# Three more landing buffers for gathered expert rows, shared with the tiles that empty the accumulators

## The chip, the core and the metric

The kernel runs on one core of a Trainium2 chip. The metric is the device time of one execution in microseconds (us), as the median of several runs. The engines are TensorE (PE in the profile), VectorE (DVE), ScalarE (ACT), GpSimd (POOL) and SyncE (SP). SP issues the plain loads and stores, POOL issues the indirect DMAs (gathers), and 16 DMA engines carry both.

## The reference

One layer of a decoder trunk over 1024 tokens of width 1024: three mixers, a product-key expert layer (PEER), a gated per-layer embedding, a final norm. The change lies in PEER, where every token has 8 x 16 = 128 chosen experts, each with an input row `u` and an output row `v` of 1024 floats:

```
def block(args):                      # 128 tokens at a time
    xb, ib, gb = args
    act = jax.nn.gelu(jnp.einsum('td,thkd->thk', xb, u[ib]), approximate=False)
    return jnp.einsum('thk,thkd->td', act * gb, v[ib])
```

`u` and `v` have 16384 rows each (64 MB).

## The kernel before

The 1024 tokens are two halves of four blocks of 128 tokens. In the first half of the program the mixers run; the `u` rows of the first half's four blocks are gathered behind the second half's mixer work. The stage that matters here comes after that and runs from about 2570 to 4266 us.

**The scattered part.** `experts_out` computes the `v` side of six blocks without a gather. For six blocks, in two passes of three, it multiplies a matrix of weights W (experts by tokens, mostly zeros) with all of `v`. A pass has three chunks of 43, 43 and 42 steps; each step `i` loads 128 rows of `v` (`raw`, tag `vr`, four buffers, L1161, 512 KB) and runs six products of 128x512 into six accumulator banks `pair` (L1165; the trace has 12 matmuls a step). While a chunk runs, `scatter` builds the W of the next one: DVE makes one-hot tiles A8, B8 (L1085) and Bs (L1097) for 8 tokens, PE multiplies them in groups of 24 small matmuls (L1064), ACT copies the product into W (L1066). A chunk has 48 such groups.

**The gathered part.** At the same time `gathered()` works on the second half of the tokens: `experts_in` gathers 128 `u` rows per token of four blocks and reduces each with the token's own vector `hft` (L1021); `experts_rows` gathers the `v` rows of the two blocks that the passes leave out and adds them up (L1038). `rows` hands out the landing buffers in turn: three of tag `ug` in the pool `up` and, in this stage, two more, `ug0` and `ug1`, in the pool `vp`. One gather is 128 rows of 4 KB, 512 KB.

**The order.** DVE keeps the order in which the code is written. In every step from the 17th on, `feed` takes the scatter's share and then 3.2 gathered rows (`RATE`), so 240 steps take the 768 gathers. PE's, ACT's, POOL's and SP's orders are chosen by the scheduler.

**The end of a pass.** `finish` copies the six accumulator banks into three tiles `es` of 4 KB a partition (L1127, ACT), then `add_block` transposes each (L1113), copies it back (L1115) and adds it to the residual (L1117), a piece per step of the next chunk. The next pass's matmuls write the same banks. The three `es` tiles have a place of their own in `vp` and are used twice in the stage, at the end of each pass.

Of the kernel before, what the change touches and what calls it, by code (L numbers as in the profile page):

```python
# [10 lines left out]
F32 = mybir.dt.float32  # L11
# [10 lines left out]
P = 128  # L22
D = 1024
# [5 lines left out]
UB = 3  # L29
# [27 lines left out]
def tile_trunk(ctx, tc, xT, pT, w_in, w_tm, w_br, w_q, keys, peer_u, peer_v,  # L57
# [5 lines left out]
    up = ctx.enter_context(tc.tile_pool(name="up", bufs=1))  # L63
# [6 lines left out]
    def nm(s):  # L70
        cnt[0] += 1
        return f"{s}_{cnt[0]}"

    def st(shape, dt=F32, tag="t", bufs=1, pool_=None):
        p = pool_ or pool["r" if tag in ("mg", "rw", "keyt") or tag.startswith("p_") else "s"]
        return p.tile(list(shape), dt, tag=tag, name=nm(tag), bufs=bufs)
# [26 lines left out]
    turn = {"pj": 0, "g": 0, "s": 0, "t": 0, "u": -1}  # L103
# [45 lines left out]
    def pj(shape=(P, T)):  # L149
        turn["pj"] = 1 - turn["pj"]  # L150
        return bank(turn["pj"], shape)
# [94 lines left out]
    def to_cols(rows, n):  # L246

        s = tmp([16, T])[0:n]
        A.copy(out=s, in_=rows)
        tp = pg((P, NC, 16))  # L250
        for c in range(NC):
            PE.transpose(tp[:, c, 0:n], s[:, c * P:c * P + P], ident[0:n, 0:n])
        return tp[:, :, 0:n]
# [94 lines left out]
    def small_rows(hf, H):  # L348
# [31 lines left out]
        def bc(t, rows=8):  # L380
            return t.unsqueeze(2).to_broadcast([rows, NC, P])
# [609 lines left out]
    def route_slots(res, pj=pg):  # L991

        for r in res:
            tp = pj((P, 2, P))
            for i in range(2):
# [2 lines left out]
                A.copy(out=t, in_=tp[:, i])  # L998
                r[2 + i] = t

    def rows(table, ii, extra):

        for s in range(P):
            turn["u"] = (turn["u"] + 1) % (len(extra) + UB)
            m = turn["u"]
            p, tag = (up, "ug") if m < UB else extra[m - UB]
            x = st([P, D], tag=tag, bufs=UB if m < UB else 1, pool_=p)
            G.indirect_dma_start(out=x, out_offset=None, in_=table,  # L1008
                                 in_offset=bass.IndirectOffsetOnAxis(ap=ii[:, s:s + 1], axis=0))
            yield s, x  # L1010

    def experts_in(hf, tb, r, hpool, extra):


        gt, ii = r[0], r[1]
        gt = gt.rearrange("p a b -> p (a b)")
        act = st([P, P], tag="act", bufs=1, pool_=up)
        hft = st([P, D], tag="hft", bufs=1, pool_=hpool)
        SY.dma_start(out=hft, in_=hfd[hf, tb])
        for s, ug in rows(peer_u, ii, extra):  # L1020
            V.tensor_tensor_reduce(out=ug, in0=ug, in1=hft, scale=1.0, scalar=0.0,  # L1021
                                   op0=ALU.mult, op1=ALU.add, accum_out=act[:, s:s + 1])
            if s == P - 1:
                A.activation(out=act, in_=act, func=AF.Gelu)
                V.tensor_tensor(out=gt, in0=act, in1=gt, op=ALU.mult)
                r.append("weighted")
            yield

    def experts_rows(r, extra, sums):

        gt, ii = r[0].rearrange("p a b -> p (a b)"), r[1]
        o = st([P, D], tag="hft", bufs=1, pool_=up)
        sums.append(o)
        for s, vg in rows(peer_v, ii, extra):
            if s == 0:
                V.tensor_scalar(out=o, in0=vg, scalar1=gt[:, 0:1], scalar2=None, op0=ALU.mult)
            else:
                V.scalar_tensor_tensor(out=o, in0=vg, scalar=gt[:, s:s + 1], in1=o, op0=ALU.mult, op1=ALU.add)  # L1038
            yield
# [64 lines left out]
    def add_block(vp, hf, tb, e, xt=None):  # L1104

        src = xmd[hf, :, :, tb * P:tb * P + P].rearrange("k p t -> p k t")
        if xt is None:
            xt = vp.tile([P, KT, P], F32, tag="vr", name=nm("xt"), bufs=VB)
            SY.dma_start(out=xt, in_=src)
        for d in range(2):  # L1110
            tp = pj((P, NC, P))
            for k in range(4):
                PE.transpose(tp[:, k, :], e[:, d * T + k * P:d * T + k * P + P], ident)  # L1113
            f = e[:, d * T:d * T + T].rearrange("p (k t) -> p k t", k=NC)
            A.copy(out=f, in_=tp)  # L1115
            yield
            V.tensor_tensor(out=xt[:, 4 * d:4 * d + 4], in0=f, in1=xt[:, 4 * d:4 * d + 4], op=ALU.add)  # L1117
        SY.dma_start(out=src, in_=xt)
        yield

    def finish(vp, blocks, acc):

        es = []
        for b in range(3):
            e = vp.tile([P, D], F32, tag="es", name=nm("es"), bufs=3)
            for d in range(2):
                A.copy(out=e[:, d * T:d * T + T], in_=acc[b][d])  # L1127
            es.append(e)
        yield
        for e, (hf, tb) in zip(es, blocks):  # L1130
            yield from add_block(vp, hf, tb, e)

    def tile_w(n):
        return [pool[p].tile([P, (QM, CHUNKS[0][1] - QM)[k], 3 * P], F32, tag=f"W{k}", name=nm("W"), bufs=1)
# [2 lines left out]
    def experts_out(vp, W, passes, gen, then, last):  # L1137
# [7 lines left out]
        for n, (p, c) in enumerate(chunks):  # L1145
# [33 lines left out]
            if c == len(CHUNKS) - 1:  # L1179
                end = finish(vp, [x[0:2] for x in passes[p]], acc)  # L1180
                next(end)
# [54 lines left out]
    def opened(name, side="left"):  # L1236
        es = ExitStack()
        return es, es.enter_context(tc.tile_pool(name=name, bufs=1, side=side, reuse_waits="tile"))
# [109 lines left out]
    v2, vp = opened("v2", "right")  # L1348
# [3 lines left out]
    sums = []  # L1352

    def gathered():
        ex = [(vp, "ug0"), (vp, "ug1")]
        yield from experts_in(1, 0, r1[0], vp, ex)
        yield from experts_in(1, 1, r1[1], vp, ex)
        yield from experts_in(1, 2, r1[2], vp, ex)
        yield from experts_rows(r1[2], ex, sums)
        yield from add_block(vp, 1, 2, sums[0])  # L1360
        yield from experts_in(1, 3, r1[3], vp, ex)
        yield from experts_rows(r1[3], ex, sums)

    es = []
# [24 lines left out]
    blocks = [[(0, tb, r0[tb]) for tb in range(3)], [(0, 3, r0[3]), (1, 0, r1[0]), (1, 1, r1[1])]]  # L1389
    with tc.manual_schedule(engines={mybir.EngineType.DVE}):  # L1390
        experts_out(vp, W, blocks, gathered(), then, last())
        for _ in add_block(vp, 1, 3, sums[1]):
            pass
# [98 lines left out]
```

## Time and profile before

| what | us |
|---|---|
| time, median of three runs | 4431.17 |
| the three runs | 4431.17, 4423.65, 4438.31 |
| the profiled execution's own time | 4443.27 |
| its span from first to last instruction | 4441.4 |
| PE busy in the span | 4001.2 |
| DVE busy | 3306.1 |
| POOL busy | 1679.9 |
| ACT busy | 1176.4 |

The mean granted TensorE clock is 0.944 of full speed. The profile reads 1018.30 MB moved by DMA, 671.17 MB of it on the gathers' queue. The span is 1.9 us shorter than the time of its execution, which itself lies 12.1 us above the median. Busy shares are averages over stages with different limits; matmuls are pipelined, so a busy PE is not a PE at its peak.

### The profile page before, as it was taken

To read this page: it belongs to the slowest core of one execution; us is meant where nothing else is said; L and a number is where in the kernel's file an instruction comes from. 1 tells how busy PE (TensorE), PEld (TensorE's weight loads), DVE (VectorE), ACT (ScalarE), POOL (GpSimd) and SP (SyncE) were. 2 spreads that over 40 slices of the span, in tenths; PEclk is the share of its full clock that TensorE was granted. 3 is DMA by queue.
4 is the path that set the end of the run, shared out by engine and by line. 5 is a ranking of instruction groups with operands and counts; after the bars stand their busy time and mean duration, and the time that the engine had idled before them with its cause. 6 is when DMAs were issued, how large, how long until landed. Compare 5 with 4: busy or idle time off the path is not lost.

```text
span 4441.4 us, 55491 instructions
## 1 busy us (share of the span) xinstructions
PE 4001.2 (90%) x20506; PEld 2492.5 (56%) x20506; DVE 3306.1 (74%) x6607; ACT 1176.4 (26%) x2192; POOL 1679.9 (38%) x1299
## 2 busy tenths in 40 slices
PE   8999999999778988898978998999999999998967
PEld 5677787777556655556744744444444444443435
DVE  5333346549999777878879899888888888886755
ACT  3343425432325412314403201111111111110023
POOL 0000000000146665564460005566666666665620
PEclk9999999999889998899999999999999999999988
DMA  2212122242268898887783237899998999999953
GB/s 92 93 56 72 55 95 72 85 138 91 100 233 303 292 347 281 282 308 277 242 316 132 84 124 268 312 343 347 337 335 319 354 336 338 331 340 380 365 196 102
DMA packets 326081, 1018.30 MB, mean 229 GB/s; under 512 B 33584, under 2 KB 81072, under 8 KB 325552
## 3 DMA queue, kind: packets, MB, share of 16 engines
q0 software_dynamic: 184320, 671.17, 42.3%
q1 hardware_dynamic: 141488, 343.58, 22.1%
q8 instruction: 161, 2.64, 0.2%
q14 instruction: 112, 0.92, 0.1%
HBM read 992.84 MB, written 21.77 MB: 228 GB/s over the span
## 4 chain that ended last, share of the span: by engine, by line
DVE 18%; issue 17%; PE 16%; DMA 14%; POOL 10%; ACT 1%; SPq 0%; POOLq 0%; DVEq 0%; ACTq 0%
POOL ug L1008 10%; DMA ug<-in_peer_u_dram,ii 7%; PE bank L214 6%; DVE ug L1021 5%; DMA ug<-in_peer_v_dram,ii 5%; PE pair L1165 3%; DVE A L1085 1%; DVE hft L1038 1%; DVE Bs L1097 1%; PE bank L205 1%; DVE p_pk L940 1%; DVE mg L936 1%; DVE wlo L183 1%; PE pair L1064 1%; PE bank L1064 1%
## 5 line engine op out<-in xcount | busy, mean ns | idle before, releaser
L1008 POOL DMA_INDIRECT ug<-in_peer_u_dram,ii x1024 | 1348.3, 1317 | 2386.3 <-DVE ii L979 1387.5
L1165 PE MATMUL pair<-vr,W 128*128 128x512 f32 x3072 | 1414.3, 612 | 17.7 <-DMA vr<-in_peer_v_dram 17.7
L1021 DVE CUSTOM_DVE_ANT_0 ug<-ug,hft 128x1024 f32<-128x1024 f32 x1024 | 1226.4, 1220 | 272.1 <-DMA ug<-in_peer_u_dram,ii 240.3
L1165 PEld LDWEIGHTS pair<-vr,W 128*128 128x128 f32 x3072 | 579.4, 195 | 672.5 <-issue 651.7
L214 PE MATMUL bank<-hi,wlo 128*128 128x512 f32 x1552 | 623.9, 402 | 35.9 <-DVE wlo L183 34.8
L214 PE MATMUL bank<-hi,whi 128*128 128x512 f32 x1552 | 632.5, 409 | 12.2 <-ACT hi L182 4.2
L214 PE MATMUL bank<-lo,whi 128*128 128x512 f32 x1552 | 623.0, 402 | 0.1
L183 DVE TENSOR_TENSOR wlo<-raw,whi 128x1024 fp32r<-128x1024 f32 (+1 forms) x276 | 327.2, 1186 | 336.4 <-ACT whi L182 318.4
L182 ACT CAST whi<-raw 128x1024 fp32r<-128x1024 f32 (+1 forms) x276 | 282.2, 1023 | 1057.8 <-PE bank L214 618.9
L1066 ACT COPY W<-bank 128x176 f32<-128x176 f32 x480 | 179.7, 482 | 1043.6 <-PE bank L1064 980.4
L1008 POOL DMA_INDIRECT ug<-in_peer_v_dram,ii x256 | 327.8, 1280 | 190.2 <-DVE hft L1038 115.1
L1038 DVE SCALAR_TENSOR_TENSOR hft<-ug,gt,hft 128x1024 f32<-128x1024 f32 x254 | 326.1, 1284 | 86.9 <-DMA ug<-in_peer_v_dram,ii 82.1
L1064 PEld LDWEIGHTS <-A 128*128 128x128 bf16 x6912 | 212.8, 98 | 266.2 <-DVE Bs L1097 138.8
L214 PEld LDWEIGHTS bank<-hi,wlo 128*128 128x128 f32 x1552 | 296.2, 191 | 114.6 <-DVE wlo L183 45.2
L214 PEld LDWEIGHTS bank<-hi,whi 128*128 128x128 f32 x1552 | 296.2, 191 | 104.1 <-issue 27.7
L214 PEld LDWEIGHTS bank<-lo,whi 128*128 128x128 f32 x1552 | 296.8, 191 | 73.7 <-issue 12.0
L1064 PE MATMUL bank<-Bs,A 128*128 128x43 bf16 (+1 forms) x5760 | 186.5, 184 | 92.8 <-DVE Bs L1097 89.3
L1085 DVE TENSOR_TENSOR A<-iota,i 128x1024 bf16<-128x1024 bf16 x288 | 197.5, 686 | 11.1 <-PE bank L1064 9.5
L205 PE MATMUL bank<-Y,raw 128*128 128x512 f32 x384 | 179.4, 624 | 27.6 <-DVE p L839 18.4
L1097 DVE TENSOR_TENSOR Bs<-B,w 128x1032 bf16<-128x1032 bf16 (+1 forms) x288 | 198.9, 690 | 5.6
L205 PEld LDWEIGHTS bank<-Y,raw 128*128 128x128 f32 x384 | 75.3, 200 | 125.6 <-issue 88.7
L329 PE MATMUL pair<-whi,hi 128*128 128x512 f32 x256 | 102.7, 401 | 8.8 <-ACT mg L332 6.6
(429 smaller groups left out, 4469.9 us busy)
## 6 DMA issues: line engine op xcount, KB each, us to landing
vr<-in_peer_v_dram SPq DMA_DIRECT2D x256, 512.0 KB
raw<-in_w_in_dram SPq DMA_DIRECT2D x154, 512.0 KB
raw<-in_w_br_dram SPq DMA_DIRECT2D x64, 512.0 KB
raw<-in_w_tm_dram SPq DMA_DIRECT2D x32, 512.0 KB
raw<-in_w_q_dram SPq DMA_DIRECT2D x32, 512.0 KB
ug<-in_peer_u_dram,ii POOLq DMA_INDIRECT x1024
raw<-in_w_pg_dram SPq DMA_DIRECT2D x14, 512.0 KB
Y<-in_xT_dram SPq DMA_DIRECT2D x16, 256.0 KB
```

Of the source, the lines that this page charges most:

```text
L182: A.copy(out=hi, in_=src)
L183: V.tensor_tensor(out=lo, in0=src, in1=hi, op=ALU.subtract)
L205: PE.matmul(o, lhsT=raw[:, k, :], rhs=X[k] if isinstance(X, list) else X[:, k, :], start=k == 0, stop=k == nk - 1)
L214: PE.matmul(o, lhsT=l[:, k, :], rhs=r[k], start=i == 0, stop=i == n - 1)
L1008: G.indirect_dma_start(out=x, out_offset=None, in_=table, in_offset=bass.IndirectOffsetOnAxis(ap=ii[:, s:s + 1], axis=0))
L1021: V.tensor_tensor_reduce(out=ug, in0=ug, in1=hft, scale=1.0, scalar=0.0, op0=ALU.mult, op1=ALU.add, accum_out=act[:, s:s + 1])
L1038: V.scalar_tensor_tensor(out=o, in0=vg, scalar=gt[:, s:s + 1], in1=o, op0=ALU.mult, op1=ALU.add)
L1064: PE.matmul(wp_[:, u, 0:nk], lhsT=A8[:, a, :, o], rhs=Bs[:, k, a, :, o], start=k == 0, stop=k == 2)
L1066: A.copy(out=W[k][:, 0:hi - lo, b * P + t:b * P + t + 8].rearrange("p i t -> p t i"), in_=wp_[:, :, lo:hi])
L1085: V.tensor_tensor(out=o, in0=iota2[:, k0:k0 + n].unsqueeze(1).to_broadcast([P, 4, n, 2]), in1=x[:, t:t + 8].rearrange("p (a o) -> p a o", ...
L1097: V.tensor_tensor(out=Bs, in0=B8.unsqueeze(1).to_broadcast([P, 3, 4, nk, 2]), in1=w3[:, t // 8].rearrange("p k (a o) -> p k a o", o=2).uns ...
L1165: PE.matmul(acc[b][d], lhsT=l[:, b * P:b * P + P], rhs=raw[:, d * T:d * T + T], start=i2 == 0, stop=i2 == P - 1)
```

## The change

The three `es` tiles lose their own place. They are allocated under the tags `ug0`, `ug1`, `ug2`, one buffer each, and `gathered()` may use five tags, `ug0` to `ug4`, as landing buffers, in the same amount of memory. A set `lent` keeps the two uses apart: `finish` puts a tag in it before it takes the tile, `rows` steps over lent tags, and the tag returns when its block has been added.

```
+    lent = set()
+
     def rows(table, ii, extra):
 
         for s in range(P):
-            turn["u"] = (turn["u"] + 1) % (len(extra) + UB)
-            m = turn["u"]
-            p, tag = (up, "ug") if m < UB else extra[m - UB]
+            while True:
+                turn["u"] = (turn["u"] + 1) % (len(extra) + UB)
+                m = turn["u"]
+                p, tag = (up, "ug") if m < UB else extra[m - UB]
+                if tag not in lent:
+                    break
...
         for b in range(3):
-            e = vp.tile([P, D], F32, tag="es", name=nm("es"), bufs=3)
+            lent.add(f"ug{b}")
+            e = vp.tile([P, D], F32, tag=f"ug{b}", name=nm("es"), bufs=1)
...
-        for e, (hf, tb) in zip(es, blocks):
-            yield from add_block(vp, hf, tb, e)
+        for b, (hf, tb) in enumerate(blocks):
+            yield from add_block(vp, hf, tb, es[b])
+            lent.discard(f"ug{b}")
...
-        ex = [(vp, "ug0"), (vp, "ug1")]
+        ex = [(vp, f"ug{i}") for i in range(5)]
```

The sequences on PE, SP and DVE are the same instructions in the same order, but for the buffers that DVE's row operations name. On POOL, at the start of the stage, these are the first gathers with what each waits for; a plain `ug_` is one of the three in `up`, a `ug_` with a first number one of `ug0` onwards. Before:

```order
L1008 DMA ug_2816_18325<-in_peer_u_dram,ii_17859 128x1024 [waits DMASW2_49,PE_49,Activation_49]
L1008 DMA ug_18400<-in_peer_u_dram,ii_17859 128x1024 [waits DMASW3_49]
L1008 DMA ug_18403<-in_peer_u_dram,ii_17859 128x1024 [waits DMASW4_49]
L1008 DMA ug_18406<-in_peer_u_dram,ii_17859 128x1024 [waits DMASW5_49,DVE_49]
L1008 DMA ug_2832_18451<-in_peer_u_dram,ii_17859 128x1024 [waits DMASW6_49,DVE_49]
L1008 DMA ug_2833_18454<-in_peer_u_dram,ii_17859 128x1024 [waits DMASW7_49,DVE_49]
L1008 DMA ug_18457<-in_peer_u_dram,ii_17859 128x1024 [waits DMASW0_49,DVE_49]
```

The same seven gathers in the change:

```order
L1013 DMA ug_2816_18325<-in_peer_u_dram,ii_17859 128x1024 [waits DMASW2_49,PE_49,Activation_49]
L1013 DMA ug_2824_18400<-in_peer_u_dram,ii_17859 128x1024 [waits DMASW3_49]
L1013 DMA ug_2825_18403<-in_peer_u_dram,ii_17859 128x1024 [waits DMASW4_49,PE_49]
L1013 DMA ug_2826_18406<-in_peer_u_dram,ii_17859 128x1024 [waits DMASW5_49]
L1013 DMA ug_18451<-in_peer_u_dram,ii_17859 128x1024 [waits DMASW6_49]
L1013 DMA ug_18454<-in_peer_u_dram,ii_17859 128x1024 [waits DMASW7_49]
L1013 DMA ug_18457<-in_peer_u_dram,ii_17859 128x1024 [waits DMASW0_49,DVE_49]
```

The wait for DVE, which has to be done with the buffer's last row, comes with the sixth gather before and with the ninth in the change, and so on through the stage.

On ACT, at the end of the first pass, these rows empty the accumulators (`pair_68` to `pair_70`); L1066 is the copy of a scatter product into W. Before:

```order
L1127 COPY es_24923<-pair_68 128x512 [waits PE_49]
L1127 COPY es_24923<-pair_68 128x512
L1127 COPY es_24926<-pair_69 128x512 [waits PE_49]
L1127 COPY es_24926<-pair_69 128x512
L1127 COPY es_24929<-pair_70 128x512 [waits PE_49]
L1127 COPY es_24929<-pair_70 128x512
L1066 COPY W_22621<-bank_66 128x8x22 [waits PE_49]
```

The same place in the change, where L1134 is the old L1127 and L1071 the old L1066:

```order
L1134 COPY es_24923<-pair_68 128x512 [waits DVE_49,PE_49]
L1134 COPY es_24923<-pair_68 128x512
L1134 COPY es_24926<-pair_69 128x512 [waits DVE_49,PE_49]
L1134 COPY es_24926<-pair_69 128x512
L1134 COPY es_24929<-pair_70 128x512 [waits DVE_49,PE_49]
L1071 COPY W_22621<-bank_66 128x8x22 [waits PE_49]
L1071 COPY W_22622<-bank_66 128x8x21
L1071 COPY W_22621<-bank_67 128x8x22 [waits PE_49]
L1071 COPY W_22622<-bank_67 128x8x21
L1134 COPY es_24929<-pair_70 128x512
```

Each first copy now also waits for DVE, which must have used up the row that lay in that buffer, and the last copy stands behind four copies into W.

On POOL, after that pass end, these gathers (in the change) go around the lent tags; the names are given in full here:

```order
L1013 DMA ug4_3733_24894<-in_peer_u_dram,ii_2767_18025 128x1024
L1013 DMA ug_3745_24955<-in_peer_u_dram,ii_2767_18025 128x1024
L1013 DMA ug_3746_24958<-in_peer_u_dram,ii_2767_18025 128x1024
L1013 DMA ug_3747_24961<-in_peer_u_dram,ii_2767_18025 128x1024
L1013 DMA ug3_3753_25011<-in_peer_u_dram,ii_2767_18025 128x1024
L1013 DMA ug4_3754_25014<-in_peer_u_dram,ii_2767_18025 128x1024
...
L1013 DMA ug3_3779_25209<-in_peer_u_dram,ii_2767_18025 128x1024
L1013 DMA ug0_3778_25206<-in_peer_u_dram,ii_2767_18025 128x1024
L1013 DMA ug4_3780_25212<-in_peer_u_dram,ii_2767_18025 128x1024
```

Only `ug3` and `ug4` stand beside the three of `up` until `ug0` returns; counted in the full list, all eight are back in turn 36 gathers after the pass end. In that stretch three short runs of gathers are swapped by one or two places.

## Rows read from the trace of the kernel before

**Rows 1.** The chain that ended last, its shares by line.
```profile
POOL ug L1008 10%; DMA ug<-in_peer_u_dram,ii 7%; PE bank L214 6%; DVE ug L1021 5%; DMA ug<-in_peer_v_dram,ii 5%; PE pair L1165 3%; DVE A L1085 1%; DVE hft L1038 1%; DVE Bs L1097 1%; PE bank L205 1%; DVE p_pk L940 1%; DVE mg L936 1%; DVE wlo L183 1%; PE pair L1064 1%; PE bank L1064 1%
```

**Rows 2.** Windows by stage: length, busy time of PE, PEld, DVE, ACT, POOL; PEclk, DMA share, GB/s.
```profile
2680.00:2875.00 195.00, 182.88 (x1488) 91.70 (x1487) 178.19 (x329) 38.06 (x103) 119.08 (x88) 0.98 0.87 306
2875.00:4003.00 1128.00, 1051.70 (x6675) 519.88 (x6674) 951.45 (x1565) 158.81 (x424) 719.12 (x546) 0.97 0.94 338
4003.00:4266.00 263.00, 215.99 (x519) 95.84 (x517) 191.16 (x178) 17.45 (x30) 162.81 (x131) 0.92 0.99 366
```

**Rows 3.** The second of these windows, L1165 alone.
```profile
2875.00:4003.00 1128.00, 949.53 (x2048) 385.31 (x2047) 0.97 0.94 338
```

**Rows 4.** DVE's waits, 2875 to 4003: us in total, times, longest.
```profile
DVE ug L1021 <- DMA ug<-in_peer_u_dram,ii: 97.8, 101, 3.2
DVE hft L1038 <- DMA ug<-in_peer_v_dram,ii: 24.3, 27, 3.1
...
DVE ug L1021 <- DMA hft<-hfd: 9.0, 2, 4.6
```

**Rows 5.** DVE's longest wait, 2680 to 2875.
```profile
DVE ug L1021 <- DMA ug<-in_peer_u_dram,ii: 7.7, 10, 1.5
```

**Rows 6.** DVE's longest wait, 4003 to 4266.
```profile
DVE hft L1038 <- DMA ug<-in_peer_v_dram,ii: 57.8, 69, 2.6
```

**Rows 7.** PE's longest wait, 2875 to 4003.
```profile
PE bank L1064 <- DVE Bs L1097: 68.9, 32, 4.6
```

**Rows 8.** Timeline of PE, two steps without a pause: start, us, instruction.
```profile
3042.57 5.40 PE L1165 MATMUL pair<-vr,W 128*128 128x512 f32 x12
3047.80 0.76 PE L1064 MATMUL bank<-Bs,A 128*128 128x42 bf16 x24
3048.41 5.40 PE L1165 MATMUL pair<-vr,W 128*128 128x512 f32 x12
```

**Rows 9.** Groups on POOL by form, 2875 to 4003: busy, mean ns, idle before.
```profile
L1008 POOL DMA_INDIRECT ug<-in_peer_u_dram,ii x418 | 553.6, 1325 | 309.9 <-DVE act L1021 216.2 <-issue 68.2 <-DVE B L1085 13.7
L1008 POOL DMA_INDIRECT ug<-in_peer_v_dram,ii x128 | 167.5, 1308 | 99.3 <-DVE hft L1038 63.0 <-issue 17.1 <-DMA ug<-in_peer_v_dram,ii 7.8
```

**Rows 10.** Timeline of POOL: the fifth and the sixth gather of the stage.
```profile
2603.38 0.94 POOL L1008 DMA_INDIRECT ug<-in_peer_u_dram,ii  x1 [0.30 <-issue]
2680.38 1.67 POOL L1008 DMA_INDIRECT ug<-in_peer_u_dram,ii  x1 [76.07 <-DVE act L1021]
```

**Rows 11.** DMA totals, 2875 to 4003.
```profile
DMA packets 112622, 381.54 MB, mean 338 GB/s; under 512 B 11703, under 2 KB 20966, under 8 KB 112543
```

**Rows 12.** DMA totals, 4036 to 4075, in the last chunk.
```profile
DMA packets 4082, 14.82 MB, mean 380 GB/s; under 512 B 457, under 2 KB 469, under 8 KB 4080
```

**Rows 13.** Windows of 25 us, columns as in rows 2.
```profile
2925.00:2950.00 25.00, 25.00 (x172) 12.49 (x170) 21.61 (x39) 4.98 (x12) 17.15 (x13) 1.00 0.97 362
3450.00:3475.00 25.00, 18.98 (x110) 8.92 (x109) 22.17 (x41) 2.71 (x7) 16.74 (x13) 0.86 0.99 358
```

**Rows 14.** Timeline at the end of the first pass.
```profile
3422.07 1.07 ACT L1127 COPY es<-pair 128x512 f32<-128x512 f32 x2 [0.64 <-PE pair L1165]
3423.03 1.39 ACT L1066 COPY W<-bank 128x176 f32<-128x176 f32 x4
3423.26 1.22 DVE L1021 CUSTOM_DVE_ANT_0 ug<-ug,hft 128x1024 f32<-128x1024 f32 x1
```

**Rows 15.** Timeline at the end of the second pass.
```profile
4235.58 1.07 ACT L1127 COPY es<-pair 128x512 f32<-128x512 f32 x2 [0.64 <-PE pair L1165]
...
4258.73 3.69 DVE L1117 TENSOR_TENSOR xt<-es,xt 128x512 f32<-128x512 f32 x6
4262.35 3.92 DVE L1038 SCALAR_TENSOR_TENSOR hft<-ug,gt,hft 128x1024 f32<-128x1024 f32 x3
```

**Rows 16.** SP's longest wait, 2875 to 4003.
```profile
SPq L1161 <- PE pair L1165: 871.1, 145, 13.0
```

**Rows 17.** Timeline of SP and PE as the last chunk begins.
```profile
4006.77 3.69 SPq L1161 DMA_DIRECT2D vr<-in_peer_v_dram  x3
4020.80 2.07 PE L1165 MATMUL pair<-vr,W 128*128 128x512 f32 x2 [12.40 <-DMA vr<-in_peer_v_dram]
```

## The prediction

> **What bounds the kernel now.** I read the chain of waits first. The reader should see in it that no engine holds the whole program: its largest entries by line are the gathers, POOL's issue with 10% of the span and the landing of `u` and `v` rows with 7% and 5% [rows 1]. The change touches only the last large stage, so the second view is a table of windows that cuts it in three: the rest of the first chunk (2680 to 2875 us), the four middle chunks (2875 to 4003) and the last chunk with its tail (4003 to 4266) [rows 2]. The middle is the part that matters. PE, DVE and the DMA engines are all busy there and none is full: PE 1051.7 of 1128 us, DVE 951.45, DMA 0.94. The cut holds four chunks of 43, 42, 43 and 43 steps, 171 in all, which need 12 x 171 = 2052 matmuls; the trace has 2048 [rows 3].
>
> Third, DVE's waits in the middle. It is idle for 1128 - 951.45 = 176.6 us, and 97.8 + 24.3 = 122.1 us of that, 69%, is waiting for a gathered row to land [rows 4]. PE in turn waits 68.9 us for DVE's Bs tiles [rows 7]. So a late row holds DVE, which keeps its written order, and the scatter work queued behind that row comes late to PE.
>
> Why are rows late? Five buffers serve 546 rows in 1128 us [rows 9], 2.07 us a row, so a buffer goes round in 5 x 2.07 = 10.3 us. POOL has to wait for DVE to release one for 216.2 + 63.0 us [rows 9]; the start of the stage shows the limit bare, with the fifth gather issued at 2603.38 and the sixth 76 us later, when DVE has used a row [rows 10].
>
> **The change part by part.** No instruction is added or removed. Three buffers are added, two kinds of wait, and some gathers move.
>
> *Eight buffers for five.* At the present 2.07 us a row a buffer may now take 16.5 us to go round where it takes 10.3. At a pace of 1.9 us it would still have 15.2. I take the row waits of the middle as removable and ask what binds next; each bound comes from the same rows.
> - PE: two steps stand 48.41 - 42.57 = 5.84 us apart with one product group between, which itself takes 48.41 - 47.80 = 0.61, leaving 5.23 for the 12 matmuls [rows 8]. 171 x 5.23 + 192 groups x 0.61 = 1011 us.
> - DVE: 1128 - 122.1 = 1006 us if nothing else of its waits goes.
> - POOL: 546 x (1.32 + 0.30 between two issues) = 885 us [rows 9, 10].
> - DMA: 381.54 MB [rows 11] at the 366 GB/s of the last chunk [rows 2] is 1042 us; at the 380 GB/s of its best stretch [rows 12] 1004 us.
>
> PE is the nearest engine, so the most to be had is 1128 - 1011 = 117 us. That PE can run without a pause at DVE's side of the work is seen in 25 us windows where it is busy 25.00 at a granted clock of 1.00, with DVE at 21.61 [rows 13]; in a window where it stalls the clock reads 0.86, so a removed stall gives its slow restart back too. I credit the rows with their 69% share of DVE's idle time: 0.69 x 117 = 81. While tags are lent, 36 of the 546 gathers go round with five to seven buffers; that 6% is taken off: **-76 us**. This leaves the middle at 1052, just above the 1042 of the DMA bound. Lower bound of the gain 0 (rows land no earlier), upper 117.
>
> *First chunk.* DVE is nearly full (178.19 of 195) and waits 7.7 us for rows [rows 2, 5]: **-6**, between 0 and -8.
>
> *Last chunk.* DVE waits 57.8 us for rows [rows 6], but the DMA share is 0.99 with five buffers, so deeper queues mostly lengthen the landing. 263 us at 366 GB/s against the 380 GB/s of the best stretch gives 263 x (1 - 366/380) = 10 us. I take half: **-5**, between 0 and -10.
>
> *The wait before the accumulators are copied.* Each first `es` copy now waits until DVE has used the row in that buffer; behind it on ACT stand the copies into W and the casts, and PE's first matmuls of the next pass wait for the banks. At the first pass end the last eight gathers lie in three `ug`, then `ug0` to `ug4`, so the third copy needs the row that is third from last. In the trace DVE starts the last row before the end at 3423.26, so the third-last ends at about 3422.2, and ACT began its last copies at 3422.07 [rows 14]: 0.1 us. The half copy behind four W copies (1.39 us) is covered by PE, which reaches that bank five matmuls into its first step. If DVE were late by a whole turn of buffers, the cover is gone and it costs 8 x 2.07 = 16.6 us. At the second pass end the copies were done 22 us before DVE added them (4235.58 and 1.07 against 4258.73) [rows 15]. Now they follow the seventh- to fifth-last row before the end; the four rows behind, 3.92/3 = 1.31 us each [rows 15], give 5.2 us, and copy, transpose and copy take about 3. I take **+3** for both ends, between 0 and 33.
>
> *Swapped gathers and the extra PE wait of the fourth early gather.* Seven gathers move by one or two places and may cost a few us once; the early gather has 76 us to spare [rows 10]. Zero, inside the +3.
>
> The sum is -76 - 6 - 5 + 3 = -84. Against the profiled execution 4443.27 - 84 = 4359; that execution lies 12.1 above the median, so the median goes from 4431.17 to **4347**.
>
> **The rivals.**
> - *POOL becomes the bound.* A gather issued alone takes 0.94 us, one that starts just after DVE began a row takes about 1.67 [rows 10], and the mean in the middle is 1.325 [rows 9]. With DVE denser, every gather might cost 1.67 + 0.30 = 1.97: 546 x 1.97 = 1076, -52 in the middle, with the other terms -60 and 4371. For it: POOL has only the gaps. Against it: in the windows with PE full, 13 gathers took 17.15 [rows 13], 1.32 each. The Trainium skill, SBUF — State Buffer, section SBUF: two separate sides, says that some DVE operations lock GpSimd out of the port pair it needs to write descriptors; the longer gathers beside DVE rows agree with it.
> - *The DMA engines are full earlier.* At share 0.99 a middle window moved 358 GB/s [rows 13]. At that rate the middle takes 381.54/0.358 = 1066, -62, the last chunk gains nothing, and the sum is -62 - 6 + 3 = -65: 4366. The Trainium skill, DMA: Bandwidth & Descriptors, section Where 436 GB/s comes from, puts the HBM side of one core at about 358 GB/s, the same figure. The trace has 380 GB/s over 39 us [rows 12], so it is not a ceiling here.
> - *Nothing.* If rows are late because the engines are shared and not because too few are asked for, three more in flight land later by as much: 4431. For it: the last chunk waits 57.8 us at share 0.99. Against it: 0.94, and 0.87 in the first chunk, where buffers are all that is missing.
> - *Slower: PE starves for `v` loads.* SP's loads always wait for one of four buffers (871.1 us) [rows 16], so a load has 4 x 5.84 = 23.4 us to land. As the last chunk began PE resumed 14 us after loads were issued [rows 17]. Eight gathers ahead instead of five could make 14 into 22, still covered. It decides once four loads take longer than four of the present steps, 4 x 1128/171 = 26.4 us. At 28 us a step is 7.0, the middle 1197, and the time 4431 + 69 = 4500.
>
> **How the numbers follow.** The forecast gets 0.47, POOL 0.18, DMA 0.17, nothing 0.12, slower 0.06. A change of 0.3% (13 us) is about what a measurement can tell from none. The first three are faster by more than that, so faster 0.82, same 0.12, slower 0.06. The range begins at 4305, near the full PE bound with everything else (-117 - 8 - 10 = -135 gives 4296, so 2% lies below 4305) and ends at 4422, inside the "nothing" case; that leaves out 2% below and about 16% above.
>
> **What the next profile would show.** Right: DVE's waits for rows in the four middle chunks fall from 122 to under 40 us, PE's for Bs from 69 to under 30, the DMA share rises to 0.97 or more, and the cut from 2875 to 4003 shortens to about 1052 at a granted clock near 0.99. POOL's mean stays at 1.3 us; at 1.6 and a POOL without pauses, its rival holds. If row waits stay at 120 us with the share at 0.99, it is the DMA rival or nothing, by the rate. If PE waits for `vr`, the last one. A pause of PE over 5 us at the first pass end would show the lending to cost more than I allow. The prediction is wrong in its core if row waits vanish and PE still stalls as often.

## The result and the profile after

The changed kernel takes 4322.1 us as a median of four runs (4320.24 to 4324.68), the kernel before, beside it, 4434.74 (4423.65 to 4449.93): a ratio of 0.974, 95% interval 0.9719 to 0.9762, or 113 us less. The profiled execution has a span of 4322.8 us, 118.6 less than before. In a later group of runs the same file took 4339.05 against 4435.17 (0.9779, 0.9763 to 0.9796): 96 us less. The forecast was 84.

Lines of the changed kernel stand higher than before: the gather is L1013, the rows L1026 and L1043, the passes' product L1173, the load of `v` rows L1169, A and Bs L1090 and L1102, the accumulator copies L1134, the residual adds L1122.

First the table of windows, cut at the same events as before, which answers to [rows 2] (length, then busy PE, PEld, DVE, ACT, POOL; granted clock, DMA share, GB/s):

```profile
2677.00:2857.00 180.00, 177.73 (x1486) 90.54 (x1485) 175.66 (x328) 37.88 (x102) 127.21 (x88) 1.00 0.92 331
2857.00:3902.00 1045.00, 1025.37 (x6671) 510.04 (x6670) 942.82 (x1568) 157.49 (x423) 759.81 (x545) 0.99 0.97 364
3902.00:4149.00 247.00, 218.24 (x531) 97.84 (x530) 190.04 (x176) 18.15 (x32) 160.67 (x129) 0.95 1.01 391
```

The first chunk lost 15 us (195 to 180), the middle 83 (1128 to 1045), the last chunk 16 (263 to 247); the stage begins 3 us earlier and what follows it is 2 us shorter. In the middle 57 of the 83 us are PE's idle time (76 becoming 20) and 26 its busy time, at a granted clock of 0.99 for 0.97; DVE's busy time is the same to 1%, and its idle time went from 177 to 102 us. DVE's waits in the middle are next, against [rows 4] (total, times, longest):

```profile
DVE A L1090 <- PE bank L1069: 34.0, 15, 4.5
DVE wr L1084 <- ACT w L1083: 30.8, 11, 6.3
DVE ug L1026 <- DMA ug<-in_peer_u_dram,ii: 9.7, 14, 2.2
DVE ug L1026 <- DMA hft<-hfd: 7.2, 2, 4.2
```

The two row waits were 122.1 us together; the one for `u` is 9.7, and the one for `v` is no longer among the waits. In their place DVE waits for banks and casts, so for PE and for ACT behind PE. PE's two waits, against [rows 7]:

```profile
PE bank L1069 <- DVE Bs L1102: 11.5, 11, 2.6
PE pair L1173 <- DMA vr<-in_peer_v_dram: 7.5, 4, 3.4
```

The wait for Bs fell from 68.9 to 11.5. In the first chunk no row wait is left, against [rows 5]; in the last, v rows still wait, against [rows 6]:

```profile
DVE hft L1043 <- DMA ug<-in_peer_v_dram,ii: 37.3, 59, 2.6
```

POOL's two groups in the middle, against [rows 9]:

```profile
L1013 POOL DMA_INDIRECT ug<-in_peer_u_dram,ii x417 | 595.6, 1428 | 196.4 <-issue 86.3 <-DVE act L1026 78.0 <-DVE B L1090 16.1
L1013 POOL DMA_INDIRECT ug<-in_peer_v_dram,ii x128 | 165.4, 1292 | 89.1 <-DVE hft L1043 54.4 <-issue 21.9 <-DVE hft L1041 6.4
```

POOL's wait for DVE to release a buffer fell from 216.2 to 78.0 us at the `u` rows, and each `u` gather became a little dearer (1325 to 1428 ns; a `v` gather 1308 to 1292). The chain that ended last says the same: POOL's share of it fell from 10% to 6%, the landing of `u` rows from 7% to 3%, and PE's products rose from 3% to 14% [rows 1] (the page breaks the line off at its end).

```profile
PE pair L1173 14%; PE bank L214 8%; DVE ug L1026 6%; POOL ug L1013 6%; DMA ug<-in_peer_u_dram,ii 3%; DMA ug<-in_peer_v_dram,ii 2%; PE bank L1069 2%; DVE hft L1043 2%; DVE Bs L1102 1%; DVE A L1090 1%; PE bank L205 1%; DVE p_pk L940 1%; DVE m
```

### The profile page after: what moved, and what is told of

Read it like the earlier page. It is cut to its first block, busy times and chain, and to the rows that moved or that the text cites. A ratio compares the mean times of both kernels' runs of the same rounds, so it can differ in the third digit from the quotient of the medians.

```text
span 4322.8 us, 55490 instructions
## 1 busy us (share of the span) xinstructions
PE 3967.2 (92%) x20506; PEld 2482.3 (57%) x20506; DVE 3294.4 (76%) x6607; ACT 1175.5 (27%) x2192; POOL 1733.1 (40%) x1299
## 4 chain that ended last, share of the span: by engine, by line
PE 29%; DVE 20%; issue 11%; DMA 7%; POOL 6%; ACT 1%; SPq 0%; POOLq 0%; DVEq 0%; ACTq 0%
PE pair L1173 14%; PE bank L214 8%; DVE ug L1026 6%; POOL ug L1013 6%; DMA ug<-in_peer_u_dram,ii 3%; DMA ug<-in_peer_v_dram,ii 2%; PE bank L1069 2%; DVE hft L1043 2%; DVE Bs L1102 1%; DVE A L1090 1%; PE bank L205 1%; DVE p_pk L940 1%; DVE mg L936 1%; DVE wlo L183 1%; DVE B L1090 1%
## 5 line engine op out<-in xcount | busy, mean ns | idle before, releaser
L1013 POOL DMA_INDIRECT ug<-in_peer_u_dram,ii x1024 | 1403.7, 1371 | 2238.7 <-DVE ii L979 1385.7
L1173 PE MATMUL pair<-vr,W 128*128 128x512 f32 x3072 | 1390.0, 603 | 25.3 <-DMA vr<-in_peer_v_dram 25.3
L1026 DVE CUSTOM_DVE_ANT_0 ug<-ug,hft 128x1024 f32<-128x1024 f32 x1024 | 1216.0, 1220 | 158.2 <-DMA ug<-in_peer_u_dram,ii 139.2
L1173 PEld LDWEIGHTS pair<-vr,W 128*128 128x128 f32 x3072 | 569.7, 192 | 665.5 <-issue 636.8
L1071 ACT COPY W<-bank 128x176 f32<-128x176 f32 x480 | 179.5, 484 | 954.8 <-PE bank L1069 926.6
L1013 POOL DMA_INDIRECT ug<-in_peer_v_dram,ii x256 | 325.5, 1271 | 166.9 <-DVE hft L1043 82.8
L1043 DVE SCALAR_TENSOR_TENSOR hft<-ug,gt,hft 128x1024 f32<-128x1024 f32 x254 | 325.9, 1283 | 42.6 <-DMA ug<-in_peer_v_dram,ii 37.3
L1090 DVE TENSOR_TENSOR A<-iota,i 128x1024 bf16<-128x1024 bf16 x288 | 197.4, 685 | 38.2 <-PE bank L1069 34.8
L1102 DVE TENSOR_TENSOR Bs<-B,w 128x1032 bf16<-128x1032 bf16 (+1 forms) x288 | 198.5, 689 | 5.5
```

The lines of the kernel that those rows point to most:

```text
L1013: G.indirect_dma_start(out=x, out_offset=None, in_=table, in_offset=bass.IndirectOffsetOnAxis(ap=ii[:, s:s + 1], axis=0))
L1071: A.copy(out=W[k][:, 0:hi - lo, b * P + t:b * P + t + 8].rearrange("p i t -> p t i"), in_=wp_[:, :, lo:hi])
L1090: V.tensor_tensor(out=o, in0=iota2[:, k0:k0 + n].unsqueeze(1).to_broadcast([P, 4, n, 2]), in1=x[:, t:t + 8].rearrange("p (a o) -> p a o", ...
L1102: V.tensor_tensor(out=Bs, in0=B8.unsqueeze(1).to_broadcast([P, 3, 4, nk, 2]), in1=w3[:, t // 8].rearrange("p k (a o) -> p k a o", o=2).uns ...
L1173: PE.matmul(acc[b][d], lhsT=l[:, b * P:b * P + P], rhs=raw[:, d * T:d * T + T], start=i2 == 0, stop=i2 == P - 1)
```

## The experiments

My theory: the buffers make rows come in time, and then PE is the nearest bound in the middle and the DMA engines in the last chunk. The rivals: the DMA engines hold the middle too; something else than depth gives the gain; the lending or the `v` loads cost something that the gain hides.

To compare many runs, each stage is cut by events that every kernel has: the first gather that waits for a buffer, the 96th and the 288th Bs instruction (whole us, by counting them in windows from the start), and the end of the span. All times in us; the first chunk here ends, and the last begins, some 11 us before the cuts above.

| kernel | waiting gather | 96th Bs | 288th Bs | first chunk | middle | 288th to end | median |
|---|---|---|---|---|---|---|---|
| before | 2680 | 2863 | 3992 | 183 | 1129 | 449 | 4434.7 |
| after | 2677 | 2846 | 3892 | 169 | 1046 | 431 | 4322.1 |
| after, again | 2682 | 2853 | 3908 | 171 | 1055 | 432 | 4339.1 |
| six buffers | 2682 | 2853 | 3919 | 171 | 1066 | 445 | 4364.0 |
| seven | 2673 | 2842 | 3887 | 169 | 1045 | 428 | 4324.5 |
| five, lent | 2676 | 2855 | 3988 | 179 | 1133 | 460 | 4441.9 |
| three `vr` | 2680 | 2850 | 3902 | 170 | 1052 | 439 | 4335.8 |
| PE less, eight | 2675 | 2847 | 3873 | 172 | 1026 | 422 | 4304.5 |
| PE less, five | 2674 | 2851 | 3972 | 177 | 1121 | 449 | 4423.5 |
| loads spread | 2691 | 2862 | 3916 | 171 | 1054 | 431 | 4337.2 |
| 3.4 rows a step | 2686 | 2864 | 3942 | 178 | 1078 | 420 | 4354.1 |
| eight, five at the end | 2685 | 2855 | 3912 | 170 | 1057 | 459 | 4370.7 |
| PE and DVE less | 2674 | 2835 | 3797 | 161 | 962 | 431 | 4226.0 |
| PE and `vr` less | 2682 | 2855 | 3868 | 173 | 1013 | 398 | 4271.4 |

The kernels ran in three groups (six to three `vr`; PE less to 3.4 rows; the last three with "after, again"), with the kernel before at 4433.1, 4439.2 and 4435.2 in them. The changed kernel itself moved by 17 us between two groups, and its middle by 9: a smaller difference between rows of two groups tells nothing by itself.

**How many buffers?** Six, then seven:

```
-        ex = [(vp, f"ug{i}") for i in range(5)]
+        ex = [(vp, f"ug{i}") for i in range(3)]
```
```
-        ex = [(vp, f"ug{i}") for i in range(5)]
+        ex = [(vp, f"ug{i}") for i in range(4)]
```

> Six landing buffers instead of eight (ug0 to ug2 beside the three ug; all three are lent at a pass end, so three remain there). Two theories. If a buffer's trip keeps the 10.3 us that it took with five (prediction), six serve a row every 10.3/6 = 1.72 us, less than the 1.91 us a row (1045/546) at which the kernel with eight goes through the middle: then six give nearly all of the 113 us, less some 20 us for the stretch with three buffers, so about 4340. If rows come late in bursts, or the trip grows with what is asked for, each buffer gives its part: a third of 113, so about 4397, up to 4415 with the dearer lending.

> Seven landing buffers (four remain while three are lent). By the first theory of the run with six: within 10 us of eight, 4322 to 4332. By the second: two thirds of 113, about 4360. A time below that of eight would say that the eighth only adds to the queue of the DMA engines.

Measured: six 4364.0 (ratio 0.9846, 0.9814 to 0.9878), seven 4324.5 (0.9771, 0.9736 to 0.9807). Against the kernel before in their group (4433.1) the first extra buffer is worth 69 us, the second 40, and the third nothing that shows: seven and eight have the same middle. With six DVE still waits for rows in the middle:

```profile
DVE ug L1026 <- DMA ug<-in_peer_u_dram,ii: 57.8, 58, 2.8
```

Neither theory holds for six: 4364 lies between 4340 and 4397, so the mean trip of a buffer (six at 1066/546 = 1.95 us a row are 11.7 us) does not tell the need. That rows come late now and then, and so ask for one buffer more, would explain it; no run shows that. For seven the first theory was right.

**The lending alone.** Five buffers, with the accumulators emptied into two of them and a third tile:

```
-        ex = [(vp, f"ug{i}") for i in range(5)]
+        ex = [(vp, "ug0"), (vp, "ug1")]
```

> Five landing buffers as before, but the accumulators are emptied into ug0, ug1 and a third tile, so two of the five are lent at a pass end: the lending alone, without more depth. If rows are late for want of buffers, 12 gathers with three buffers and 12 with four cost 12 x (10.3/3 - 2.07) + 12 x (10.3/4 - 2.07) = 22 us at the first pass end, about 25 us over the kernel before in all: 4460. If lending costs nothing there and buffers are not what rows wait for: 4435. Over 4480 would mean that the copies of the accumulators wait for rows far longer than the +3 us of the prediction allows.

Measured: 4441.9, a ratio of 1.0022 (1.0006 to 1.0039), so 9 us dearer where 22 to 25 were expected. The middle, with the first pass end in it, took 4 more and the stretch behind it 10 (span 4447.5 - 3988 against 4441.4 - 3992). The second pass end shows why: ACT's copies wait for rows that come late there, and PE's transposes wait for the copies (total, times, longest):

```profile
ACT es L1134 <- DMA ug<-in_peer_v_dram,ii: 41.5, 1, 41.5
...
PE bank L1118 <- ACT es L1134: 22.8, 1, 22.8
```

**The loads of `v` for PE.** Three buffers for four (`VB` = 3), eight for the gathers:

```
-LAG, RATE, VB = 16, 3.2, 4
+LAG, RATE, VB = 16, 3.2, 3
```

> Eight landing buffers, and three instead of four for the rows of v that PE multiplies (VB 3). The slower rival of the prediction says that these loads are near starving: with three a load has 3 x 5.23 = 15.7 us to land. If it holds in part, PE waits for vr all along and the time is 4370 or more. If the 6.9 us that a load takes to land is all, only the start of the last chunk suffers, where PE waits 16.6 us for vr behind 17.65 us of other loads on SP: one buffer less adds 5.2 us, so about 4328.

Measured: 4335.8 (0.9778, 0.9742 to 0.9813). The middle has 1052 us, as with four (1046 and 1055). PE's wait for `vr` at the start of the last chunk grew from 16.6 to 21.9 us, by as much as was expected. Its waits for `vr` from 2855 us on (total, times, longest):

```profile
PE pair L1173 <- DMA vr<-in_peer_v_dram: 35.1, 6, 21.9
```

So PE is not near starving for these loads, and the slower rival is out.

**Is PE the bound?** One of the six products of a step left out, with eight buffers and with five:

```
                     for d in range(2):
+                        if i2 and (b, d) == (2, 1):
+                            continue
                         PE.matmul(acc[b][d], lhsT=l[:, b * P:b * P + P], rhs=raw[:, d * T:d * T + T],
-                                  start=i2 == 0, stop=i2 == P - 1)
+                                  start=i2 == 0, stop=i2 == P - 1 or (b, d) == (2, 1))
```

> Eight landing buffers, and one of the six products of a step left out in 127 of 128 steps (the last half block of each pass keeps only its first step's product, so that part of the output lacks the rest). It takes 2 of 12 matmuls, 5.23/6 = 0.87 us a step, 149 us over the 171 steps of the middle. If PE's work is what bounds the middle with eight buffers (it is busy 1025 of 1045 us there), the middle falls until DVE stands against it, busy 943 us and with some 40 us of waits: to about 985, and the time to about 4250. If the DMA engines are the bound at share 0.97, or rows are still late, the middle stays near 1045 and the time within 20 us of 4322.

> The kernel before, five landing buffers, with the same product left out. If late rows bind the middle there (a buffer goes round in 10.3 us, 2.07 us a row, whatever PE does), it stays within 15 us of 1129 and the time within 20 us of 4433, however much PE is relieved. If PE was the bound before too and the deeper queue helps in another way, it falls as much as with eight buffers, by 60 to 80 us.

Measured: 4304.5 with eight (0.9707, 0.9681 to 0.9733) and 4423.5 with five (0.9966, 0.995 to 0.9982). The middles as windows, eight above, five below:

```profile
2847.00:3873.00 1026.00, 913.42 (x6364) 452.80 (x6364) 943.79 (x1572) 158.71 (x427) 752.21 (x544) 0.94 0.98 375
```
```profile
2851.00:3972.00 1121.00, 938.54 (x6364) 457.36 (x6364) 952.70 (x1573) 160.50 (x428) 725.13 (x545) 0.94 0.95 344
```

With five buffers 114 us less work on PE shortened the middle by 8: late rows held it, whatever PE did. DVE's row waits there are 105.8 and 27.0 us, as many as before:

```profile
DVE ug L1021 <- DMA ug<-in_peer_u_dram,ii: 105.8, 108, 3.3
DVE hft L1038 <- DMA ug<-in_peer_v_dram,ii: 27.0, 26, 3.7
```

With eight, 113 us less work on PE gave 20 by these marks, not the 60 that I expected if PE alone bounds it. But here the marks no longer part the same work. As the last chunk nears, SP issues 16 small loads ahead of the next `v` rows. In the changed kernel they come from 3893.3 us on, just behind the 288th Bs, and the 16.6 us that PE then waits for `vr` hold no Bs. With PE relieved they come at 3827.1, 46 us ahead of the 288th Bs; PE waits 20.0 us for `vr` behind them, and DVE waits 19.0 us for PE, both inside the middle (total, times, longest):

```profile
PE pair L1175 <- DMA vr<-in_peer_v_dram: 37.7, 10, 20.0
DVE A L1090 <- PE bank L1069: 26.7, 4, 19.0
```

Without these 19 us the middle has 1007, 39 us less than 1046 (with five buffers the like wait holds DVE for 1.9 us only). Something else stands some 40 us behind PE: DVE (943.79 busy of 1026, with 6.5 us of waits for rows) or the DMA engines (share 0.98). The next pair tells which. Both leave out the same product; one also does the row operations of the second half of the tokens on half the columns, the other loads half of each `v` row:

```
+            w = slice(0, T if hf else D)
-            V.tensor_tensor_reduce(out=ug, in0=ug, in1=hft, scale=1.0, scalar=0.0,
+            V.tensor_tensor_reduce(out=ug[:, w], in0=ug[:, w], in1=hft[:, w], scale=1.0, scalar=0.0,
...
-                V.scalar_tensor_tensor(out=o, in0=vg, scalar=gt[:, s:s + 1], in1=o, op0=ALU.mult, op1=ALU.add)
+                V.scalar_tensor_tensor(out=o[:, 0:T], in0=vg[:, 0:T], scalar=gt[:, s:s + 1], in1=o[:, 0:T],
+                                       op0=ALU.mult, op1=ALU.add)
```
```
-                SY.dma_start(out=raw, in_=pv[:, i2, :])
+                SY.dma_start(out=raw[:, 0:T], in_=pv[:, i2, 0:T])
...
-                        PE.matmul(acc[b][d], ..., rhs=raw[:, d * T:d * T + T],
+                        PE.matmul(acc[b][d], ..., rhs=raw[:, 0:T],
```

> Eight landing buffers, one of six products left out as in the run before, and every row operation of the second half of the tokens on 512 of 1024 columns (what they add up lacks the other half). PE then has some 880 us of work in the middle and DVE some 640, and the same 385 MB move. If the DMA engines at share 0.98 stopped the run with PE relieved at 1026 us, the middle stays near 1026 (375 GB/s). If it was DVE, at 944 us busy and its waits on PE and ACT, the middle falls to what the DMA engines can do at the 400 to 410 GB/s of the last chunk: 940 to 963 us, and the time to about 4230.

> Eight landing buffers, one of six products left out as before, and each load of v rows cut to its first 512 columns, used for both halves (so the second half of the passes' output is that of the first): 45 MB less in the middle, 340 for 385. If the DMA engines stopped the run with PE relieved at 1026 us, the middle falls with them to about 950 to 975 us, where DVE stands (944). If DVE and what it waits for did, the middle stays within 10 us of 1026 and the DMA share falls to about 0.88.

Measured: 4226.0 (0.9526, 0.9508 to 0.9543) and 4271.4 (0.9639, 0.9623 to 0.9655). The middles, DVE relieved above, `v` loads below:

```profile
2835.00:3797.00 962.00, 902.28 (x6337) 454.40 (x6337) 663.63 (x1572) 154.83 (x426) 567.94 (x543) 0.98 1.01 395
```
```profile
2855.00:3868.00 1013.00, 907.67 (x6364) 449.35 (x6362) 942.61 (x1571) 158.34 (x426) 762.61 (x544) 0.95 0.94 336
```

With the bytes unchanged (380 MB) and DVE relieved the middle falls to 962, from 1026 or, without the 19 us, 1007; the 16 loads come right at the mark again there (3797.3). With DVE unchanged and 45 MB less it has 1013, of which the same wait behind the 16 loads holds DVE for 12.0 us: 1001, so 6 less than 1007. I had expected the DMA share to fall to 0.88 there; it fell from 0.98 to 0.94 only, with as many packets (114875 and 114865), so this run relieves the DMA engines less than its bytes say. Together the two show that DVE with its hand-overs to PE and ACT stood behind PE, and the DMA engines farther off. At 962 these are the nearest bound: their rate in 40 equal slices of that stretch lies flat at 408 to 409 GB/s for long runs of slices, and DVE waits for rows again (44.9 and 25.2 us). PE is not far behind them, with 902 us busy:

```profile
GB/s 355 384 406 393 405 388 408 408 409 409 407 408 400 352 405 404 393 408 408 371 301 400 350 382 409 408 409 408 409 408 380 394 409 404 368 406 408 408 408 408
```

The order with eight buffers is thus PE at about 1046, DVE some 40 us behind, the DMA engines some 45 behind that. No run relieves DVE alone; that PE alone holds 1046 rests on its being busy 1025 of 1045 us there and on the fall when it is relieved.

**What holds the last chunk?** Two runs. One deals out the 16 loads that SP issues there ahead of the `v` rows; the other goes back to five landing buffers when the last chunk begins:

```
-                if n == len(chunks) - 1 and i % 2 == 1:
+                if n == len(chunks) - 1 and (i % 2 == 1 or i < 16):
...
+            if p2 is None:
+                yield
```
```
-    lent = set()
+    lent, deep = set(), []
...
                         pool["banks"] = [0, 1]
+                        del deep[2:]
...
-        ex = [(vp, f"ug{i}") for i in range(5)]
+        ex = deep
+        ex.extend((vp, f"ug{i}") for i in range(5))
```

> Eight landing buffers, and the 16 small loads that SP issues in 17.65 us at the start of the last chunk are dealt out two a step over eight steps. PE waits 16.6 us for vr there, right behind these loads. If SP's queue is the cause, the wait goes and the time falls by 10 to 17 us, to about 4308. If the last chunk is bound by the DMA engines (410 GB/s over its length), the rows and loads end at the same time whatever the order, and it stays within 5 us of 4322.

> Eight landing buffers up to the last chunk, and from its start five (ug2 to ug4 are no longer handed out). The stretch from the 288th Bs to the end took 449 us before and 431 after. If depth is what raised the DMA engines there from 366 to 400 GB/s, it goes back: about 448 us, and the time to about 4339. If the last chunk gained because the chunks ahead of it left less over (rows and loads in a better order), it stays near 431 and the time near 4322.

> The changed kernel itself once more, beside the other three on one chip. The profiles so far put the first gather that waits for a buffer between 2673 and 2692 us in kernels that are the same up to there, so the time before the stage moves the total by some 15 us from run to run. If that is all, 4322 within 15 us, with the middle (96th to 288th Bs) at 1046 within 6 us.

Measured: 4337.2 with the loads dealt out (0.977, 0.9745 to 0.9794), 4370.7 with five buffers at the end (0.9854, 0.9837 to 0.987), 4339.1 for the same kernel again (0.9779, 0.9763 to 0.9796). The same kernel again missed what I expected of it by a little: 17 us above 4322 where I allowed 15, and a middle of 1055 for 1046. Beside it, dealing out the loads moved nothing: PE's wait for `vr` fell from 16.6 us in one to 11.3 in four, and the stretch from the 288th Bs to the end stayed at 431. The going back cost 27 us in that stretch (432 to 459) and nothing ahead of it. The windows from the 288th Bs to the last row, same kernel again above, five at the end below:

```profile
3908.00:4166.00 258.00, 227.87 (x599) 102.94 (x597) 198.82 (x191) 20.83 (x38) 169.65 (x134) 0.95 1.01 389
```
```profile
3912.00:4198.00 286.00, 233.15 (x599) 105.49 (x597) 198.37 (x191) 20.92 (x37) 167.83 (x136) 0.90 0.95 351
```

The rate fell from 389 to 351 GB/s with the depth (and with lending among five). Of the 27 us some 18 are what the last chunk gained by the change (449 to 431); the rest resembles the 10 us that lending among five buffers cost there, and PE's transposes again wait for the copies (18.6 us). SP's order of the loads was not the bound, the DMA engines were: where PE and DVE were relieved and the bytes kept, this stretch stayed at 431, and where half of each `v` load was left out beside PE's product, it fell to 398. PE is full in the steady part too (busy 75.00 us from 4025 to 4100), but leaving out its product alone gave 422 only, and there 5 MB more had moved ahead of the stretch.

**More rows a step.**

```
-LAG, RATE, VB = 16, 3.2, 4
+LAG, RATE, VB = 16, 3.4, 4
```

> Eight landing buffers and 3.4 rows a step for 3.2: 34 more rows in the 171 steps of the middle, as many fewer in the last chunk. If PE bounds the middle, its 1045 us take the rows in (DVE 943 + 34 x 1.25 = 985), the last chunk is left to PE with 42 x 5.23 + 16.6 = 236 us for 247, and the time falls by about 10, to 4312. If the middle is at the limit of the DMA engines (364 GB/s at share 0.97), 17.8 MB more cost it 49 us and give some 40 back: 4330.

Measured: 4354.1 (0.9811, 0.979 to 0.9833), slower than the kernel with 3.2. The last chunk gained 11 us as expected, but the middle went to 1078, 23 to 32 more:

```profile
2864.00:3942.00 1078.00, 1033.64 (x6690) 510.22 (x6689) 987.55 (x1615) 160.47 (x427) 792.44 (x578) 0.98 0.98 370
```

DVE's row waits stayed small there (4.0 us for `v` rows and 2.9 for `u`), so it is not the DMA engines, which the second theory named. DVE has 43 us more work and is now the nearer engine together with its waits for PE and ACT. That the two, working in one written order, cannot both be full would explain it; that is argued, not shown.

## Why the prediction was right, and where it was short

*Rows were late for want of buffers.* Shown three ways: row waits fell from 122 to 10 us, freeing PE did little with five buffers (1129 to 1121), and each of the first two extra buffers shortened the middle (1129, 1066, 1045).

*The middle, -76.* Measured -83, within the bounds of 0 and 117. The marks that the prediction set are met: row waits under 40, PE's wait for Bs under 30 (11.5), share 0.97, clock 0.99; 1045 us for 1052. That the credit of 69% of the room up to PE's bound came out close is in part luck, two errors against each other. PE was busy 1025 us where I worked out 1011 (I had left out 43 transposes, 8.4 us, and that the clock is not full throughout), so the room was 103 us and not 117; and 83 of these, 81%, came. Of the other bounds, DVE's 1006 is near the 1007 found with PE relieved, and the 1004 to 1042 of the DMA engines were too high, as 962 shows.

*The first chunk, -6, at most -8.* Measured -15, and this step failed. I counted only the waits that name a row (7.7 us). With the rows in time, DVE's waits for PE and ACT shrank as well, from 6.4 to 3.1 us: its idle time there went from 195 - 178.19 = 16.8 to 180 - 175.66 = 4.3 us, its busy time by 2.5, and PE's clock from 0.98 to 1.00. That those waits followed from the late rows is argued, not shown. Part of the 15 may be chance: between the marks of the table the first chunk took 183 us before, but 179 and 177 in the two other profiles with five buffers, against 169 and 171 in the two of the changed kernel.

*The last chunk, -5, at most -10.* Measured -16; the size failed. I took the share of 0.99 for nearly full and the best stretch of 380 GB/s for the ceiling, and halved what that gave. With eight buffers the chunk moves 391 GB/s. Its steady part, 4025 to 4100, holds this:

```profile
DMA packets 8435, 30.71 MB, mean 409 GB/s; under 512 B 946, under 2 KB 946, under 8 KB 8431
```

*The pass ends, +3.* The first is free: the copies waited 1.2 us for a row and PE had no wait between 3330 and 3375. The timeline of ACT:

```profile
3353.90 1.07 ACT L1134 COPY es<-pair 128x512 f32<-128x512 f32 x2 [1.20 <-DVE act L1026]
3355.47 1.07 ACT L1134 COPY es<-pair 128x512 f32<-128x512 f32 x2 [0.49 <-PE pair L1173]
```

At the second I priced the copies, and the price lies elsewhere: the last gathers take tags that come back only when DVE has added their block, and POOL waits for that:

```profile
4136.34 0.93 POOL L1013 DMA_INDIRECT ug<-in_peer_v_dram,ii  x1 [9.84 <-DVE xt L1122]
4139.50 0.94 POOL L1013 DMA_INDIRECT ug<-in_peer_v_dram,ii  x1 [2.23 <-DVE xt L1122]
```

The last two rows then land 2.60 and 1.74 us late, 4.3 us in all, near the 3 that I allowed.

*The rivals.* POOL's gathers rose to 1428 ns, not to 1670, and POOL has 196.4 + 89.1 us idle in the middle: not the bound. The Trainium skill, SBUF — State Buffer, section SBUF: two separate sides, speaks of a lock between some DVE and GpSimd work; the trace agrees by the times of its records, see below, and no run here shows the lock itself. The DMA engines' 358 GB/s is refuted by 409. "Nothing" fell with the row waits, and the slower rival with three `vr` buffers.

As a whole the forecast was short: its terms sum to -84, and the parts of the profile to -3 - 15 - 83 - 16 - 2 = -119. Of the 35 us between, 9 and 11 are the first and the last chunk, 7 the middle, 3 the pass ends, which are inside these stretches, and 5 lie outside the stage, where the time differs between runs of equal code by more than that.

## What to carry to other kernels

Where an engine that keeps its order waits for gathered data, ask how many transfers are in flight before asking how busy the DMA engines are: a busy share of 0.94 to 0.99 was no limit here, two buffers more gave 109 us where three gave 113 and, measured again, 96. Buffers that are idle between rare events can be lent for this at almost no price, but only when rows come in time; with five buffers the same lending made the copies wait. And a wait for rows has echoes: count the idle time that follows from it on the engine that waits and on the one behind it, not only the wait that names the row. Last, where a run relieves an engine, look whether the marks that cut its stages still part the same work: here a wait of 20 us had moved across one.

## What the runs showed of the hardware that I had not expected

**The DMA share says little near 1.** The last chunk moved 366 GB/s at a share of 0.99 with five gathers in flight, 391 at 1.01 with eight, and 409 in its steady part. The Trainium skill, Perfetto Trace Analysis, section Identifying the Most-Contended Engine, says that with 16 DMA engines their occupancy misleads and that HBM utilization is to be used instead; the trace agrees, as the rate at a share of 1.03, that of the steady part, is 12% above the rate at 0.99.

**A gather that starts inside a DVE row operation ends 0.81 us after that operation.** Beside nothing it takes 0.94 us [rows 10]. In the middle with eight buffers 227 gathers stand by themselves in the timeline and start while DVE runs an L1026; 215 of them end 0.75 to 0.88 us after that operation's end, and the other 12, which start in its first 0.04 us, take 0.94. One pair of records, DVE until 2999.34 and POOL until 3000.16:

```profile
2998.13 1.21 DVE L1026 CUSTOM_DVE_ANT_0 ug<-ug,hft 128x1024 f32<-128x1024 f32 x1
2998.16 2.00 POOL L1013 DMA_INDIRECT ug<-in_peer_u_dram,ii  x1 [0.30 <-issue]
```

It fits that the mean rose with a denser DVE (1325 to 1428 ns), and that shorter operations let it fall. With the row operations cut to half their columns (1220 to 687 ns at L1026) POOL's means in the middle fell, from 1412 and 1298 ns with only PE relieved, to these, near 0.94 us:

```profile
L1013 POOL DMA_INDIRECT ug<-in_peer_u_dram,ii x415 | 430.0, 1036 | 302.3 <-DVE act L1027 188.7 <-issue 82.1 <-DVE B L1092 8.0
L1013 POOL DMA_INDIRECT ug<-in_peer_v_dram,ii x128 | 138.0, 1078 | 93.0 <-DVE hft L1044 55.8 <-issue 18.3 <-DVE hft L1042 8.8
```

**A PE with gaps is granted less clock.** With one of six products left out PE has work for less of the middle (913 of 1026 us), and its granted clock there is 0.94 (a mix of the two levels, 1.2 and 2.4 GHz) instead of 0.99. Its busy time fell by 113 us, where the products left out are, by an estimate from [rows 8] at full clock, 149 us. With DVE relieved too, PE is busy 902 of 962 us, and the clock reads 0.98.
